# Two plain gate/value pairs instead of three ahead of the Strassen products, and operand-sum words that go through DRAM

## The chip, the core and the metric

The kernel runs on one core of a Trainium2 chip. A core has five engines, each with its own instruction queue: TensorE (PE in the profile, with its weight loads as PEld), VectorE (DVE), ScalarE (ACT), GpSimd (POOL) and SyncE (SP), which here only issues transfers. Engines wait for each other through semaphores. A transfer (DMA) is started by an instruction in an engine's queue and moved by sixteen DMA engines. Matrix products end in PSUM, everything else that the engines read lies in the on-chip memory SBUF, and what doesn't fit there goes to DRAM.

The metric is the time of one execution in microseconds, the median of the runs.

## What is computed

One step of a decoder layer for two groups of requests together: a prompt of 1024 tokens and 8 x 8 sample tokens, so 1088 tokens (T) with a model width of 1024. Cut to what bears on the change, the end of the layer is:

```python
    h = x + merged @ w_out
    up = rmsnorm(h, norm2_g) @ w_up                 # 1024 -> 2 * 2816
    up_ext = jnp.concatenate([conv_f_past, up], axis=1)
    uc = dwconv_valid(up_ext, ffn_conv_w, ffn_conv_b)   # depthwise, 3 steps in time
    gate, val = jnp.split(uc, 2, axis=-1)
    y = h + (jax.nn.silu(gate) * val) @ w_down
```

with `rmsnorm(x, g) = x * rsqrt(mean(x * x) + eps) * g`. Attention, the convolution branch and the input projection come before and are not touched. All of it is fp32.

## The kernel before, in words

**Products.** TensorE multiplies in a reduced format (fp32r), so each fp32 factor is split into a high and a low part, and a product is three matmuls: high weight by high operand, high weight by low operand, low weight by high operand (`mm3`, L188 to L192, which is why the matmuls of the profile stand at L190, L191 and L192). The split is `split_ps` (L224 to L226): ScalarE casts the value into the high part, then VectorE subtracts that from the value to get the low part. Weights come in raw (`wraw`, 512 KB each, loaded on SP's queue by `w_load`) and are split by `w_parts` (L171 on ScalarE, L172 on VectorE) into tiles `whi` and `wlo`.

**The norm.** The output stage (`out`) works in four quarters of 272 tokens (`QUARTERS`). As each quarter of h is finished, `norm2(c)` (L1071) makes one matmul for the mean of squares (L1074), the reciprocal root, and then, for each of eight slices k of 128 model channels, the normed value `nt` (VectorE, L1080; three rotating tiles of 128 x 272) and its split into `mh` (high) and `ml` (low). At its end POOL's queue stores the quarter of h to DRAM (`d_h`). The last quarter's norm is placed 42 priority steps late (`NORM_LATER`), so that it falls inside the first pair of the next stage. The pool `wt`, in which `nt` lies, is closed behind it, and its memory is then free for the pools of the next stage.

**The up stage** (`ffn_up`, L1102) has 22 pairs: the gate unit f and the value unit f, each 128 channels wide. The first `PLAIN` = 3 pairs are plain: two units by four quarters by eight slices by three matmuls, each 272 columns wide, 192 matmuls. The other pairs (`pair`, L1291) take the 2 x 2 block product of Strassen and Winograd with the two weights as one side and two halves of the tokens and of the channels as the other: seven products, each of 24 matmuls, 168. For these, both sides need sums. The operand sums T1 to T4 are made once, by `sums()` (L1222), in four rounds (two halves j by two slices kk). A round builds four words of 128 x 544 in the four rotating tiles `s` (`word`), each of which is the norm's value of two slices for one quarter; then four VectorE operations combine them, and four splits put them in the tiles `th` and `tl`. Before the change, `word` is a VectorE addition that puts the value together again from `mh` and `ml`. `sums()` is called behind the first plain pair, `SUM_LATER` = 60 priority steps late.

The weight sums of a pair are made by `preps` (`plan_pair`, L1250): seven steps a pair, each an optional VectorE sum (L1264, into the same `s` tiles) and a split into one of four ring tiles named `whi0`, `wlo0`, `whi1`, `wlo1` (each holds a high and a low half of 128 x 512). They run three products ahead (`AHEAD`). The seven products use in turn the operands "11", T1, T2, "22", T3, "21", T4.

**Behind a pair**, `finish` (L1175) works on what ScalarE has copied from PSUM into `st` (L1163): `up_conv` writes the edges of the convolution's state with POOL copies, starts the sum on ScalarE (L1170) and adds the two other steps on VectorE (L1172, twice a unit); then Silu, gate times value (L1182, L1185), and a store to DRAM for the down stage (`d_g`, or the parts `d_b` with their differences). The argument `late` of `finish` is in priority steps; the plain pairs pass 0, the others `UP_LATER` = 100, and gate times value another `GATE_LATER` = 60.

**Order.** The program is written in one order and each engine's queue is filled by a scheduler that goes by priority; `later(n)` makes what stands under it n steps less urgent. So a change in one place can move instructions of another engine. Transfers of weights and `word`s wait in SP's queue, in order; stores (`d_h`, `d_g`, `d_b`) and the copies of the key and value caches (`o_kwp`, `o_vwp`, 960 KB each, in `up_start` of unit 2) in POOL's queue, in order. A rotating tile is given again when its last reader is done; a tile in memory that another pool had before waits for that pool's last users, transfers among them.

`raw_slot` and `slot` place weights: the raw weights of every other pair behind the plain ones go to `wraw2`, and the two halves of the last plain unit's weight (the one just before `first`, which follows from `PLAIN`) are put in `wraw2` too, the others in `whi` and `wlo`. The pool `ft`, which holds `wraw2`, `s`, `st` and `acc`, is opened when `wt` is closed.

Of the kernel before, what the change touches and what calls it, by code (L numbers as in the profile page):

```python
# [6 lines left out]
F32 = mybir.dt.float32  # L7
F32R = mybir.dt.float32r
AF = mybir.ActivationFunctionType
ALU = mybir.AluOpType  # L10
AX = mybir.AxisListType

P = 128
DM = 1024
KT = DM // P
# [21 lines left out]
AW = FW - 2  # L37
QW = T // 4
QUARTERS = [(c * QW, QW) for c in range(4)]
PLAIN = 3  # L40
AHEAD = 3
UP_LATER = 100
SUM_LATER = 60
GATE_LATER = 60
DOWN = ((0, 1), (2, 3), (16, 17), (18, 19, 20, 21))
# [75 lines left out]
class Build:  # L121
# [475 lines left out]
    def run(self):  # L597
        nc, tc, a = self.nc, self.tc, self.a
        es = ExitStack()
        with es:  # L600
            dp = es.enter_context(tc.tile_pool(name="dram", bufs=1, space=bass.MemoryType.DRAM))
            self.d_ah = self.t(dp, [4, P, T], "d_ah")
            self.d_al = self.t(dp, [4, P, T], "d_al")
            self.d_c = self.t(dp, [KT, P, T], "d_c")
            self.d_ga = self.t(dp, [KT, P, T], "d_ga")
            self.d_gb = self.t(dp, [KT, P, T], "d_gb")
            self.d_ma = self.t(dp, [KT, P, T], "d_ma")
            self.d_h = self.t(dp, [KT, P, T], "d_h")
            self.d_g = self.t(dp, [NF, P, T], "d_g")
            self.d_b = self.t(dp, [6, 7, P, HALF], "d_b")  # L610
            self.psum = es.enter_context(tc.tile_pool(name="psum", bufs=4, space=bass.MemoryType.PSUM))
            g = es.enter_context(tc.tile_pool(name="g", bufs=1))
            self.wp = es.enter_context(tc.tile_pool(name="w", bufs=2))
            self.consts = self.t(g, [P, CTOT], "consts")
            first = COFF["ident"][0]
            nc.scalar.dma_start(self.consts[:, :first], a["consts"][:, :first])
            self.ident = self.c("ident", 0, P)
            self.mean = self.t(g, [P, P], "mean")
            self.identr = self.t(g, [P, P], "identr", F32R)
            nc.vector.memset(self.mean, 1.0 / DM)  # L620
            self.warm = self.t(g, [P, 1], "warm")
            nc.vector.memset(self.warm, 1.0)
            self.nsink = self.t(g, [P, 16], "nsink")
            self.cb2 = self.t(g, [P, KT], "cb2")
            self.hsum = self.t(g, [P, KT * 16], "hsum")
            self.nsrow = self.t(g, [P, 2], "nsrow")
            ps = self.bank("mm")
            for _ in range(12):
                nc.tensor.matmul(ps[:, 0:P], self.mean, self.mean, start=True, stop=True)
            self.w_raw, self.w_hl, self.w_used, self.w_stop = [], [], 0, len(self.order)  # L630
            self.phase_x()
# [361 lines left out]
    def phase_z(self, s_es, sh, sl):  # L993
        nc, tc, a, pool = self.nc, self.tc, self.a, self.pool
        m_es = ExitStack()
        mp = pool(m_es, "m")

        def quarters():
            make = lambda x: [[self.t(mp, [P, KT // 2, QW], f"m{x}{c}{y}", F32R) for y in range(2)] for c in range(4)]
            return make("h"), make("l")  # L1000

        mh, ml = quarters()
        z_es = ExitStack()
        zt = pool(z_es, "zt")

        def xs(c, k):
            return sh[c][:, k, :], sl[c][:, k, :]

        def do_pb(m):
            t = self.t(zt, [P, T], "gb", bufs=2)  # L1010
            nc.sync.dma_start(t, self.d_gb[m])
            nc.scalar.activation(t, t, AF.Sigmoid)
            r = self.t(zt, [P, T], "mar", bufs=2)
            nc.sync.dma_start(r, self.d_ma[m])

            def ev(c, o, n, ps):
                cs = slice(o, o + n)
                nc.vector.tensor_tensor(t[:, cs], ps[:, :n], t[:, cs], ALU.mult)
                nc.vector.tensor_tensor(r[:, cs], r[:, cs], t[:, cs], ALU.add)
                for z, (qo, qn) in enumerate(QUARTERS):  # L1020
                    lo, hi = max(o, qo), min(o + n, qo + qn)
                    if lo < hi:
                        d = slice(lo - qo, hi - qo)
                        self.split_ps(mh[z][m // 4][:, m % 4, d], ml[z][m // 4][:, m % 4, d], r[:, lo:hi])

            self.stream(("pb", m), xs, ev)

        for m in range(KT):
            do_pb(m)
        z_es.close()  # L1030
        s_es.close()
        h_es = ExitStack()
        hp = pool(h_es, "h", "left")
        H = self.t(hp, [P, KT, T], "H")
        wb = pool(h_es, "wb", "left")
        wt_es = ExitStack()
        wt = pool(wt_es, "wt")
        ssq = [self.t(wt, [P, QW], f"ssq{c}") for c in range(4)]
        n_out = self.order.index(("out", 0))
        tail = n_out + KT - OUT_TAIL  # L1040

        def slot(i):
            if i < n_out:
                return self.wp, i % 2
            if tail <= i < tail + OUT_TAIL:
                return wt, f"t{i - tail}"
            if i >= tail + OUT_TAIL:
                return self.wp, i % 2
            return ((self.wp, 1), (wb, 0), (self.wp, 0))[(i - n_out) % 3]

        self.slot = slot

        def xm(c, k):
            return mh[c][k // 4][:, k % 4, :], ml[c][k // 4][:, k % 4, :]

        def ev_out(m):
            def ev(c, o, n, ps):
                t = self.t(wt, [P, QW], "xr2", bufs=4)
                nc.sync.dma_start(t[:, :n], a["xT"][m, :, o:o + n])
                hs = H[:, m, o:o + n]  # L1060
                nc.vector.tensor_tensor(hs, ps[:, :n], t[:, :n], ALU.add)
                if m == 0:
                    nc.scalar.activation(ssq[c][:, :n], hs, AF.Square)
                else:
                    nc.scalar.activation(t[:, :n], hs, AF.Square)
                    nc.vector.tensor_tensor(ssq[c][:, :n], ssq[c][:, :n], t[:, :n], ALU.add)
            return ev

        hh, hl = [], []

        def norm2(c):  # L1071
            o, n = QUARTERS[c]
            ps = self.bank("aux")
            nc.tensor.matmul(ps[:, :n], self.mean, ssq[c][:, :n], start=True, stop=True)  # L1074
            self.rstd(ssq[c][:, :n], ps[:, :n])
            hh.append([self.t(mp, [P, KT // 2, QW], f"mh{c}{y}", F32R) for y in range(2)])
            hl.append([self.t(mp, [P, KT // 2, QW], f"ml{c}{y}", F32R) for y in range(2)])
            for k in range(KT):
                t = self.t(wt, [P, QW], "nt", bufs=3)
                nc.vector.scalar_tensor_tensor(t[:, :n], H[:, k, o:o + n], self.c("g2", k), ssq[c][:, :n],  # L1080
                                               ALU.mult, ALU.mult)
                self.split_ps(hh[c][k // 4][:, k % 4, :], hl[c][k // 4][:, k % 4, :], t[:, :n])
            nc.gpsimd.dma_start(self.d_h[:, :, o:o + n].rearrange("k p t -> p k t"), H[:, :, o:o + n])

        ms = list(range(KT))
        for m in ms[:-OUT_TAIL]:
            self.stream(("out", m), xm, ev_out(m), table=QUARTERS)
        ws = [self.weight(("out", m), 2) for m in ms[-OUT_TAIL:]]
        for c in range(4):
            for m, w in zip(ms[-OUT_TAIL:], ws):  # L1090
                self.stream(None, xm, ev_out(m), chunks=(c,), w=w, table=QUARTERS)
            with self.later(NORM_LATER[c]):
                norm2(c)
        wt_es.close()
        h_es.close()
        self.gt = {}
        self.ffn_up(hh, hl, mp)
        self.ffn_down(mp)
        m_es.close()


    def ffn_up(self, hh, hl, mp):  # L1102
        nc, tc, a, pool = self.nc, self.tc, self.a, self.pool
# [101 lines left out]
        def plain(f):  # L1205
            fs = (f, NF + f)
            ws = [self.weight(("up", x), 2 - n if f == 0 else 1) for n, x in enumerate(fs)] if f == 0 else [None] * 2
            both = [up_start(x) for x in fs]
# [4 lines left out]
            else:  # L1213
                for x, b in zip(fs, both):
                    self.stream(("up", x), xs, b[3], chunks=range(4), table=QUARTERS)
            finish(f, both, 0)

        def g_raws(n):
            for f in self.groups[n]:
# [2 lines left out]
        def sums():  # L1222
            add = lambda o, x, y, op=ALU.add: nc.vector.tensor_tensor(o, x, y, op)
            for j in range(2):
                for kk in range(0, KT // 2, 2):
                    ks = slice(kk, kk + 2)

                    def word(c, y):
                        r = self.t(ft, [P, 2, QW], "s", bufs=4)
                        add(r, hh[c][y][:, ks].bitcast(F32), hl[c][y][:, ks].bitcast(F32))  # L1230
                        return r

                    r11, r12, r22, r21 = word(j, 0), word(2 + j, 0), word(2 + j, 1), word(j, 1)
# [88 lines left out]

        for f in range(PLAIN, NF):
            plan_pair(f)
# [353 lines left out]
```

## Time and profile before

| | us |
|---|---|
| time, median of three runs | 1666.21 (1664.36 to 1667.17) |
| span of the profiled execution | 1662.4 |
| TensorE busy | 1652.5 (99%) |
| VectorE busy | 1337.3 (80%) |
| ScalarE busy | 866.3 (52%) |
| GpSimd busy | 290.2 (17%) |

The page has no time of the profiled execution other than its span, the time from the first to the last instruction of the trace. TensorE's granted clock is at full speed in every slice of the span, and the DMA engines move 113 GB/s as a mean over it.

How to read the rows: a group of instructions is named by line, engine, operation, the tiles out<-in, and the shapes (partitions x elements); "x16 | 11.5, 721" means sixteen of them, 11.5 us busy together, 721 ns each. Rows of a timeline begin with the start in us from the span's start and the duration in us; several equal instructions in a row are one row, and a bracket at the end gives the idle time of the engine before it and who ended it. Rows of transfers give the size and the us from issue to landing. A matmul's duration is that of its passage through the array; the next one starts long before it is out, so the pace is read from starts.

### The profile page before, as it was taken

Reading aid. Unit: us, or ns where it says so; the run is one execution under the profiler, and the core shown is the slowest. Engines: PE = TensorE matmul, PEld = TensorE weight load, DVE = VectorE, ACT = ScalarE, POOL = GpSimd, SP = SyncE. Lnnn points to the kernel's source line nnn. Section 1 sums busy time; section 2 is a strip of 40 time slices with the busy share of each in tenths; the row PEclk is TensorE's granted clock in tenths of the full one; section 3 lists DMA queues with packets and bytes.
Section 4 is the critical chain, followed back from the end, with each engine's and each line's share of the span. In section 5 each row is a group of like instructions: output and inputs, shape, how many; then the busy total and the mean of one; then the engine's idle time right before and its main releaser. Section 6 shows DMA issues by size and latency. Waiting matters only on the chain.

```text
span 1662.4 us, 29877 instructions
## 1 busy us (share of the span) xinstructions
PE 1652.5 (99%) x11550; PEld 1636.9 (98%) x11550; DVE 1337.3 (80%) x2432; ACT 866.3 (52%) x1781; POOL 290.2 (17%) x483
## 2 busy tenths in 40 slices
PE   9999999999999999999999999999999999999998
PEld 9999999999999999999999999999999999999997
DVE  7899979999989986855545896777887786988867
ACT  6424368774488845973233454444444454524222
POOL 0100112231011111110000171344444320000000
PEclk9999999999999999999999999999999999999999
DMA  6221212232121265544343332244444324766403
GB/s 208 84 71 42 75 60 81 99 103 86 55 53 48 77 227 168 178 154 145 106 155 108 80 125 103 97 113 115 112 114 111 94 103 134 243 168 168 118 14 108
DMA packets 98623, 187.09 MB, mean 113 GB/s; under 512 B 22848, under 2 KB 57680, under 8 KB 98464
## 3 DMA queue, kind: packets, MB, share of 16 engines
q1 hardware_dynamic: 79152, 125.18, 24.3%
q0 software_dynamic: 18896, 59.72, 11.9%
q8 instruction: 91, 1.49, 0.4%
q14 instruction: 52, 0.43, 0.1%
q10 hardware_dynamic: 432, 0.27, 0.1%
HBM read 129.75 MB, written 57.35 MB: 113 GB/s over the span
## 4 chain that ended last, share of the span: by engine, by line
PE 91%; DVE 5%; ACT 2%; DMA 1%; issue 1%; ACTq 0%; DVEq 0%; SPq 0%
PE mm L190 23%; PE mm L192 23%; PE mm L191 23%; PE aux L190 6%; PE aux L192 6%; PE aux L191 6%; PE aux L406 1%; DVE c L520 1%; PE aux L418 1%; PE aux L419 1%; PE aux L396 1%; PE aux L397 1%; DVE bt L520 1%; DVE q L739 1%; DMA bw<-d_b 0%
## 5 line engine op out<-in xcount | busy, mean ns | idle before, releaser
L190 PE MATMUL mm<-xh,whi 128*128 128x384 f32 (+1 forms) x904 | 301.1, 333 | 0.0
L191 PE MATMUL mm<-xl,whi 128*128 128x384 f32 (+1 forms) x904 | 295.4, 327 | 0.1
L192 PE MATMUL mm<-xh,wlo 128*128 128x384 f32 (+1 forms) x904 | 295.4, 327 | 0.0
L191 PEld LDWEIGHTS mm<-xl,whi 128*128 128x128 f32 x904 | 170.0, 188 | 1.6 <-DVE xl L277 0.7
L190 PEld LDWEIGHTS mm<-xh,whi 128*128 128x128 f32 x904 | 169.8, 188 | 0.7
L192 PEld LDWEIGHTS mm<-xh,wlo 128*128 128x128 f32 x904 | 169.7, 188 | 0.1
L190 PE MATMUL mm<-mh,whi 128*128 128x272 f32 (+4 forms) x428 | 125.9, 294 | 0.0
L191 PE MATMUL mm<-ml,whi 128*128 128x272 f32 (+4 forms) x428 | 125.1, 292 | 0.0
L192 PE MATMUL mm<-mh,wlo 128*128 128x272 f32 (+4 forms) x420 | 123.5, 294 | 0.0
L1172 DVE SCALAR_TENSOR_TENSOR acc<-st,fc,acc 128x1104 f32<-128x1104 f32 x88 | 119.8, 1364 | 2.8 <-ACT acc L1170 2.0
L171 ACT CAST whi<-wraw 128x1024 fp32r<-128x1024 f32 (+1 forms) x76 | 74.2, 981 | 79.8 <-PE mm L191 59.7
L520 DVE SCALAR_TENSOR_TENSOR bt<-u,consts,bt 128x513 f32<-128x513 f32 x120 | 89.8, 748 | 0.7
L520 DVE SCALAR_TENSOR_TENSOR c<-sm,hsum,c 128x512 f32<-128x512 f32 x120 | 89.6, 747 | 0.7
L172 DVE TENSOR_TENSOR wlo<-wraw,whi 128x1024 fp32r<-128x1024 f32 (+1 forms) x76 | 86.1, 1136 | 4.9 <-ACT whi L171 4.6
L520 DVE SCALAR_TENSOR_TENSOR c<-u,consts,c 128x512 f32<-128x512 f32 x112 | 83.7, 747 | 0.5
L190 PEld LDWEIGHTS mm<-mh,whi 128*128 128x128 f32 x428 | 80.5, 188 | 0.2
L191 PEld LDWEIGHTS mm<-ml,whi 128*128 128x128 f32 x428 | 80.6, 188 | 0.0
L192 PEld LDWEIGHTS mm<-mh,wlo 128*128 128x128 f32 x420 | 79.0, 188 | 0.0
L1152 POOL COPY st<-co 128x16 f32<-128x16 f32 x44 | 75.6, 1724 | 0.2 <-issue 0.2
L191 PE MATMUL mm<-tl,whi 128*128 128x272 f32 x240 | 69.6, 290 | 0.0
L1320 ACT COPY st<-mm 128x272 f32<-128x272 f32 (+2 forms) x133 | 44.6, 349 | 47.8 <-PE mm L192 47.8
L192 PE MATMUL mm<-th,whi 128*128 128x272 f32 x240 | 69.3, 289 | 0.0
(462 smaller groups left out, 5491.6 us busy)
## 6 DMA issues: line engine op xcount, KB each, us to landing
wraw<-wall SPq DMA_DIRECT2D x118, 512.0 KB, 3.8
bw<-d_b SPq DMA_DIRECT2D x42, 272.0 KB, 3.4
d_b<-gd POOLq DMA_DIRECT2D x36, 272.0 KB, 6.1
d_b<-acc POOLq DMA_DIRECT2D x24, 272.0 KB, 3.3
ar<-wdn SPq DMA_DIRECT2D x32, 192.0 KB, 4.3
d_g<-acc POOLq DMA_DIRECT2D x10, 544.0 KB, 4.3
ga<-d_ga SPq DMA_DIRECT2D x8, 544.0 KB, 4.0
gb<-d_gb SPq DMA_DIRECT2D x8, 544.0 KB, 3.6
```

Of the source, the lines that this page charges most:

```text
L171: self.cast = self.nc.scalar.copy(h[:, z], r[:, z]).ins
L172: self.nc.vector.tensor_tensor(l[:, z], r[:, z], h[:, z].bitcast(F32), ALU.subtract)
L190: mm(ps, wh, xh, start=first, stop=False, skip_group_check=more)
L191: mm(ps, wh, xl, start=False, stop=False, skip_group_check=more)
L192: mm(ps, wl, xh, start=False, stop=last, skip_group_check=more)
L396: nc.tensor.matmul(ps[:, j, :], q[g][:, h, qs], kd[g][:, keys], start=True, stop=False)
L397: nc.tensor.matmul(ps[:, j, :], q[g][:, h, qs], kl[g][:, keys], start=False, stop=True)
L406: nc.tensor.transpose(ps[:, h * P:(h + 1) * P], pt[:, h, kb * P:(kb + 1) * P], self.ident)
L520: mac = lambda o, x, w: nc.vector.scalar_tensor_tensor(o, x, w, o, ALU.mult, ALU.add)
L1152: nc.gpsimd.tensor_copy(ss[:, :, 0:2], co[:, f, 2:].rearrange("p (b t) -> p b t", b=NB))
L1172: nc.vector.scalar_tensor_tensor(acc, st[:, k:k + AW], fw(f, k), acc, ALU.mult, ALU.add)
L1320: op(d, r(ps))
```

## The change

`PLAIN` goes from 3 to 2: the third pair is made by products like the others, and the Strassen pairs begin one pair earlier. `finish` of the plain pairs gets 240 priority steps instead of 0. In `norm2` the normed values are made in tiles of two slices (`nt`, 128 x 2 x 272, four of them), and behind every second slice POOL's queue stores such a tile to a new tensor in DRAM, `d_n`: four stores of 272 KB a quarter, sixteen in all. `word` no longer adds `mh` and `ml`; it loads the value from `d_n` on SP's queue into the tile `s`, sixteen loads of 272 KB. The value is then the norm's fp32 result itself and not the sum of its two parts. The four combinations and four splits of a round stay as they are.

```diff
@@ -37,9 +37,10 @@
-PLAIN = 3
+PLAIN = 2
 AHEAD = 3
 UP_LATER = 100
+PLAIN_LATER = 240
 SUM_LATER = 60
@@ -606,6 +607,7 @@
             self.d_h = self.t(dp, [KT, P, T], "d_h")
+            self.d_n = self.t(dp, [4, KT // 2, P, 2, QW], "d_n")
             self.d_g = self.t(dp, [NF, P, T], "d_g")
@@ -1076,10 +1078,13 @@
             for k in range(KT):
-                t = self.t(wt, [P, QW], "nt", bufs=3)
-                nc.vector.scalar_tensor_tensor(t[:, :n], H[:, k, o:o + n], self.c("g2", k), ssq[c][:, :n],
-                                               ALU.mult, ALU.mult)
-                self.split_ps(hh[c][k // 4][:, k % 4, :], hl[c][k // 4][:, k % 4, :], t[:, :n])
+                if k % 2 == 0:
+                    pair = self.t(wt, [P, 2, QW], "nt", bufs=4)
+                t = pair[:, k % 2, :]
+                nc.vector.scalar_tensor_tensor(t, H[:, k, o:o + n], self.c("g2", k), ssq[c][:, :n], ALU.mult, ALU.mult)
+                self.split_ps(hh[c][k // 4][:, k % 4, :], hl[c][k // 4][:, k % 4, :], t)
+                if k % 2:
+                    nc.gpsimd.dma_start(self.d_n[c, k // 2], pair)
             nc.gpsimd.dma_start(self.d_h[:, :, o:o + n].rearrange("k p t -> p k t"), H[:, :, o:o + n])
@@ -1213,7 +1218,7 @@
-            finish(f, both, 0)
+            finish(f, both, PLAIN_LATER)
@@ -1227,7 +1232,7 @@
                         r = self.t(ft, [P, 2, QW], "s", bufs=4)
-                        add(r, hh[c][y][:, ks].bitcast(F32), hl[c][y][:, ks].bitcast(F32))
+                        nc.sync.dma_start(r, self.d_n[c, (4 * y + kk) // 2])
                         return r
```

The line numbers of the prediction are those of the kernel before.

## The prediction

> **What bounds the kernel now.** I read the page's head and its chain of waits first, then TensorE's own waits from 1000 us on, then the timelines of the stretch that the change touches.
>
> ```profile
> span 1662.4 us, 29877 instructions
> PE 1652.5 (99%) x11550; PEld 1636.9 (98%) x11550; DVE 1337.3 (80%) x2432; ACT 866.3 (52%) x1781; POOL 290.2 (17%) x483
> ...
> PE 91%; DVE 5%; ACT 2%; DMA 1%; issue 1%; ACTq 0%; DVEq 0%; SPq 0%
> ```
>
> ```profile
> PE mm L190 <- DVE H L1456: 0.9, 1, 0.9
> ```
>
> TensorE is never without work: 91% of the chain that ends last is its own matmuls, and in the last 662 us it waits once, for 0.9 us. So time is won by removing matmuls and lost by each wait given to TensorE. The plain pairs and the first product of the first Strassen pair look like this in its timeline (start, duration, instruction):
>
> ```profile
> 929.90 0.29 PE L190 MATMUL mm<-mh,whi 128*128 128x272 f32 x1
> ...
> 1003.19 0.29 PE L190 MATMUL mm<-mh,whi 128*128 128x272 f32 x1
> ...
> 1006.22 0.29 PE L190 MATMUL aux<-th,wlo 128*128 128x272 f32 x1
> ```
>
> The three plain pairs (576 matmuls) run from 929.90 to 1003.19. The first product, 24 matmuls, takes 1006.22 - 1003.19 = 3.03 us, so a matmul costs 0.126 us (the 0.29 is its length in the pipeline), and 576 of them 72.6; the other 0.66 is the fourth quarter's norm matmul, run in two passes inside the first pair. VectorE has to make the operand sums T1 to T4 and the weight sums before 1006.22. It ends that work here:
>
> ```profile
> 942.61 2.62 DVE L1223 TENSOR_TENSOR s<-mh,ml 128x544 f32<-128x544 f32 x4
> 945.15 1.47 DVE L1223 TENSOR_TENSOR s<-s,s 128x544 f32<-128x544 f32 x2
> ...
> 995.19 0.68 DVE L1264 TENSOR_TENSOR s<-wraw,wraw 128x512 f32<-128x512 f32 x1
> 1007.11 0.69 DVE L226 TENSOR_TENSOR whi<-s,whi 128x512 fp32r<-128x512 f32 x1 [11.24 <-ACT whi L225]
> ```
>
> It is busy from the norm's end, 942.6, to 995.9, and then idle for 11.24 us. That is all the slack there is, and the change takes away 24.2 us of the time in which it lies.
>
> **What is removed.** A plain pair is 8 quarters of 24 matmuls, 192; a Strassen pair is 7 products of 24, 168. One pair changes from one to the other: 24 x 0.126 = 3.03 us less on TensorE. This is certain, and it is the largest gain there can be: 0.18%. VectorE loses its word additions and keeps these (view by lines, 930 to 1003 us; busy, mean ns):
>
> ```profile
> L1223 DVE TENSOR_TENSOR s<-s,s 128x544 f32<-128x544 f32 x16 | 11.5, 721 | 0.0
> L226 DVE TENSOR_TENSOR tl<-s,th 128x544 fp32r<-128x544 f32 x16 | 11.1, 722 | 0.0
> L1172 DVE SCALAR_TENSOR_TENSOR acc<-st,fc,acc 128x1104 f32<-128x1104 f32 x8 | 10.8, 1366 | 0.0
> L1223 DVE TENSOR_TENSOR s<-mh,ml 128x544 f32<-128x544 f32 x16 | 10.7, 719 | 0.0
> ...
> L1182 DVE TENSOR_TENSOR acc<-acc,acc 128x1024 f32<-128x1024 f32 x2 | 2.4, 1221 | 0.0
> ```
>
> Back to back a 128x544 operation takes (945.15 - 942.61)/4 = 0.635 us, so 16 additions are 10.2 us. Against 24.2 us of lost time that leaves 14.0 to find, of which 11.2 were idle; the rest is later convolutions (PLAIN_LATER).
>
> **What is added: a round trip through DRAM.** Sixteen stores d_n on POOL's queue, beside the four d_h; sixteen word loads on SP's queue. The nearest rows for their size (272 KB; last column us from issue to landing), and the spread of bw's loads:
>
> ```profile
> wraw<-wall SPq DMA_DIRECT2D x118, 512.0 KB, 3.8
> bw<-d_b SPq DMA_DIRECT2D x42, 272.0 KB, 3.4
> d_b<-gd POOLq DMA_DIRECT2D x36, 272.0 KB, 6.1
> d_b<-acc POOLq DMA_DIRECT2D x24, 272.0 KB, 3.3
> ```
>
> ```profile
> DMA to landing us min/median/max: 2.6/3.4/5.4
> ```
>
> The first twelve stores fall in the output stage, where each of 12 us has room (four norm2 calls, POOL 17% busy): cost 0, at most 1 us if the x loads that share the DMA engines come late. The last quarter decides. Its last norm multiply and the work behind it:
>
> ```profile
> 940.85 0.91 DVE L1080 SCALAR_TENSOR_TENSOR nt<-H,consts,ssq 128x272 f32<-128x272 f32 x2
> ...
> 953.57 1.22 DVE L172 TENSOR_TENSOR wlo<-wraw,whi 128x1024 fp32r<-128x1024 f32 x1
> ```
>
> In the built order of the changed kernel the first VectorE instruction after norm2 is the split of the last plain unit's weight into wraw2. That tile lies where the norm's nt tiles lay, so it waits for the last d_n store. Last multiply done 941.8, store landed 3.3 later: 945.1 (bounds 944.4 with 2.6, 947.9 with 6.1). Split, 1.2: 946.3. On SP's queue the load of the next wraw waits for that split, and three of the first four word loads stand behind it, though their data has long been in DRAM. 512 KB takes 3.8 in the median row and 3.5 on an idle queue (view of DMA, 940 to 960 us):
>
> ```profile
> wraw<-wall SPq DMA_DIRECT2D x2, 512.0 KB, 3.5
> ```
>
> So it lands at 949.8, and the words, half as large, about 0.8 apart behind it: 950.6, 951.4, 952.2. So VectorE idles some 2.5 + 4.3 us where it had four additions (2.5 us): nearly half of the 10.2 saved is given back in the first round.
>
> **Start of the second plain pair.** Then five sums and splits (3.2 us) and the low half of the gate weight (L172, 1.2): from 950.6 on 4.4 us without a gap, 955.0; with some 0.6 of waiting for the second and third word, 955.6. TensorE is done with the first pair at 929.90 + 0.66 + 24.2 = 954.8 and needs that low half 0.25 later: 955.0. Stall +0.6; bounds 0 (loads at 2.6) and 4 (store at 6.1 and loads at their slowest).
>
> **Start of the first product T1.** From 955.6 VectorE's order holds 26 sums and splits of 0.635 (16.5), six convolution steps L1172 of 1.28 (7.7), a gate multiply (L1182, 1.2, and its small remainder) and two weight pieces (0.7 each) ahead of T1's weight: 26.8 us, 982.4. TensorE, begun on that pair at 954.8 + 0.6, gets to T1 at 955.4 + 24.2 + 3.0 = 982.6. Just in time, were that all. But behind it stands one more L1172, of the second pair's value half, which waits for ScalarE, which waits for the last plain matmul:
>
> ```profile
> 952.75 0.44 ACT L1163 COPY st<-mm 128x208 f32<-128x208 f32 x2
> 953.28 1.31 ACT L1170 ACTIVATE acc<-st,fc 128x1104 f32<-128x1104 f32 x1
> 954.49 0.63 ACT L225 CAST th<-s 128x544 fp32r<-128x544 f32 x1
> ...
> 957.76 2.64 DVE L1172 SCALAR_TENSOR_TENSOR acc<-st,fc,acc 128x1104 f32<-128x1104 f32 x2
> 960.32 0.72 DVE L1223 TENSOR_TENSOR s<-s,s 128x544 f32<-128x544 f32 x1
> ...
> 1060.47 0.29 PE L192 MATMUL mm<-th,whi 128*128 128x272 f32 x1
> 1060.80 0.62 ACT L225 CAST whi<-s 128x512 fp32r<-128x512 f32 x1 [2.40 <-PE mm L192]
> 1061.46 0.69 DVE L226 TENSOR_TENSOR whi<-s,whi 128x512 fp32r<-128x512 f32 x1 [0.15 <-ACT whi L225]
> ```
>
> Two steps of L1172 take 960.32 - 957.76 = 2.56, so one is 1.28. ScalarE begins 1060.80 - 1060.47 = 0.33 after the start of the matmul it waits for. The last plain matmul starts 3.0 before T1 is due, at 979.6; then the copy, L1170, a th cast and the weight's cast follow, 0.53 + 1.21 + 0.63 + 0.62 = 3.0 us, so the high half is there at about 982.9 (+0.3). VectorE, free at 982.4, does L1172 (1.28), the last tl (0.64) and the low half (0.69): 985.0, wanted after four matmuls of the high half, 983.4. Stall 0.3 + 1.6 = +1.9, set by the order, hardly by the loads (bounds 1.2 to 2.2).
>
> To this comes what the later word rounds lose. Four s buffers hold one round, so each load waits until its predecessor's word has been split. Rounds 2 and 4 are covered by convolution steps. Round 3 issues at 962 to 966 and meets the cache copies (view of DMA, 960 to 975 us):
>
> ```profile
> o_kwp<-kpT POOLq DMA_DIRECT2D x1, 960.0 KB, 7.2
> o_vwp<-vp POOLq DMA_DIRECT2D x1, 960.0 KB, 10.6
> d_g<-acc POOLq DMA_DIRECT2D x1, 544.0 KB, 9.5
> wraw<-wall SPq DMA_DIRECT2D x1, 512.0 KB, 4.2
> ```
>
> A load of 512 KB took 4.2 us at their end, 3.8 elsewhere. VectorE comes to round 3 at about 968.4. I take +1.0; bounds 0 (all landed) and 4.6 (words only when o_vwp is done, 973).
>
> **In the second Strassen pair** the built order of TensorE runs product "21" directly after T1, not T2. Both weights use the same ring tile (whi0), so TensorE must stand until T1's last matmul is out, the cast (0.62) is done and, four matmuls later, the low half (0.69) too. By the rows above: 0.33 + 0.62 - 0.13 = 0.8, and 0.3 more for the low half (0.15 + 0.69 less four matmuls, 0.5). +1.1 (0.9 to 1.4). The later pairs keep their old order: 0.
>
> **Sum**: -3.0 + 0.6 + 1.9 + 1.0 + 1.1 = +1.6 us; best ends -3.0 + 0 + 1.2 + 0 + 0.9 = -0.9, worst ends together -3.0 + 4 + 2.2 + 4.6 + 1.4 = +9.2. The profiled span goes from 1662.4 to 1664.0; the median of the runs lies 3.8 above that span, and I keep this distance: 1666.2 + 1.6 = **1667.8 us**.
>
> **Rivals.** (1) The stalls are hidden and the matmuls count in full: 1663.2 to 1665. For it: 11.24 us of idle VectorE. Against: T1's low half stands behind work that waits for the last plain matmul, whatever the loads do. (2) Late words: round 3's loads land only as o_vwp ends. From the point where they land after 968.4, each us later is a us on T1: up to 4.6 instead of 1.0, +5.2 in all, 1671.4; with the first round slow as well, 1674. For it: 10.6 and 9.5 us in that window. Against: SP's 512 KB took 4.2. (3) The last d_n store is slow, as d_g's was (9.5 us instead of 3.3): the split, the loads and the second plain pair start 6.2 later, about 3 to 6 of it stay: 1670 to 1673. For it: that d_g was issued at 964.5, amid VectorE's sums. Against: VectorE has 0.8 us of work left and then waits for this very store.
>
> [...]
>
> **How the numbers follow.** Forecast as summed, -0.9 to +3.3: 0.53. Rival 1: 0.13. Rival 2: 0.24. Rival 3: 0.08. Anything else: 0.02. A measurement of this kernel can tell 0.2%, 3.3 us, from no change. Rival 1 hardly gets there (3.0), so faster 0.04; slower takes rivals 2 and 3 and the rest, 0.34; same 0.62. The range leaves out the ends of rival 1 and the worst sums: 1664.8 to 1672.5; the forecast's own is 1665.3 to 1669.5.
>
> **What would show it.** Right: 24 fewer matmuls; TensorE waits for the gate weight near 955 (under 1 us), for wlo at T1 near 982 (about 2.9, round 3's share in it) and for whi after the second pair's T1 near 1008 (about 1.1); VectorE idle from 942.6 to about 950 but for one split. Wrong: no wait of TensorE in 980 to 985 (rival 1), VectorE idle near 968 for over 2 us on s loads (rival 2), or the wraw2 split starting after 947 (rival 3).

## The result, and the profile after

| | before | after |
|---|---|---|
| time, median of five runs each, us | 1665.79 (1664.36 to 1667.17) | 1674.04 (1672.96 to 1678.07) |
| ratio | | 1.0052, 95% interval 1.0040 to 1.0065 |
| span of the profiled execution, us | 1662.4 | 1676.3 |

The changed kernel is 8.25 us slower; 1667.8 was forecast, 1664.8 to 1672.5 was the range. The profiled execution of the changed kernel is the slowest of its five, 4.0 us over the median; that of the kernel before is the fastest. Spans are therefore not compared below, but places.

The page's head and chain of waits of the changed kernel:

```profile
span 1676.3 us, 29931 instructions
PE 1655.6 (99%) x11526; PEld 1639.5 (98%) x11526; DVE 1335.6 (80%) x2433; ACT 868.3 (52%) x1786; POOL 279.2 (17%) x499
...
PE 67%; issue 18%; DVE 7%; DMA 3%; ACT 2%; POOL 2%; SPq 0%; ACTq 0%; DVEq 0%; POOLq 0%
```

The 24 matmuls are gone (11550 to 11526). Yet the chain that ends last runs through TensorE for 67%, not 91%: behind T1 it goes back over a load of words and VectorE to the last d_n store, and from there along POOL's queue. These shares tell where the chain runs and not what it costs: the changed kernel with the copies in pieces, below, has 72% and the same 18% of issue, at 1664.89 us. TensorE's own waits, 900 to 1100 us (total, times, longest), in which the kernel before has none:

```profile
PE aux L191 <- ACT wlo L226: 7.3, 1, 7.3
PE aux L191 <- ACT whi L226: 0.7, 1, 0.7
PE aux L193 <- DVE wlo L227: 0.3, 1, 0.3
```

Lines are one to five numbers higher than before: L191 to L193 are the three matmuls, L226 the cast, L227 the low half. The first and third wait are at T1, the second in the second Strassen pair. TensorE's timeline shows what T1 cost, from the last matmul of the product "11" to the start of T2:

```profile
981.97 0.29 PE L193 MATMUL mm<-mh,whi 128*128 128x272 f32 x1
...
989.53 0.60 PE L191 MATMUL aux<-th,wlo 128*128 128x272 f32 x1 [7.27 <-ACT wlo L226]
...
995.84 0.43 PE L191 MATMUL mm<-th,whi 128*128 128x272 f32 x1
```

T1 was due at 981.97 + 0.13 = 982.1 and began 7.4 late. Its 24 matmuls then took 995.84 - 989.53 = 6.3 us; before, 3.0. The table by stages says why (last columns: granted clock, DMA share, GB/s):

```profile
985.00:989.50 4.50, 0.00 (x0) 0.00 (x0) 4.50 (x7) 4.16 (x9) 1.72 (x2) 0.61 0.55 215
989.50:996.00 6.50, 6.14 (x25) 5.82 (x26) 5.87 (x9) 1.55 (x4) 0.00 (x0) 0.50 0.01 4
996.00:998.00 2.00, 2.00 (x17) 2.00 (x16) 0.41 (x1) 1.93 (x6) 0.00 (x0) 0.94 0.00 0
```

While TensorE waited its clock was taken to half (1.00 over 984 to 986, 0.50 over 986 to 988), and it stayed there until some 7 us after work had come back (0.50 up to 996, 0.94 over 996 to 998): 3.3 us more on T1, in which the 0.3 for the low half lies. So T1 cost 7.4 + 3.3 = 10.7 us, the second pair 0.9, and the saved matmuls are 3.0: +8.6, against +8.25 measured.

This execution loses in one more place. In the down stage, from 1440 us on, TensorE waits 3.6 us in all (0.9 in the kernel before), and its clock is at 0.72 as a mean over 1528 to 1534, which costs 6 x 0.28 = 1.7. Together that is 4.4 us more than before, about what this execution lies over the median; no profile shows what the other four lose there.

Why T1 began late, VectorE shows:

```profile
941.81 0.86 DVE L227 TENSOR_TENSOR ml<-nt,mh 128x272 fp32r<-128x272 f32 x2
944.47 1.23 DVE L173 TENSOR_TENSOR wraw<-wraw,wraw 128x1024 fp32r<-128x1024 f32 x1 [1.81 <-DMA d_n<-nt]
950.32 1.58 DVE L1228 TENSOR_TENSOR s<-s,s 128x544 f32<-128x544 f32 x2 [4.62 <-DMA s<-d_n]
...
953.71 1.22 DVE L173 TENSOR_TENSOR wlo<-wraw,whi 128x1024 fp32r<-128x1024 f32 x1
...
967.08 1.23 DVE L1187 TENSOR_TENSOR acc<-acc,acc 128x1024 f32<-128x1024 f32 x1
974.94 0.73 DVE L1228 TENSOR_TENSOR s<-s,s 128x544 f32<-128x544 f32 x1 [6.63 <-DMA s<-d_n]
...
990.40 0.68 DVE L227 TENSOR_TENSOR wlo<-s,wlo 128x512 fp32r<-128x512 f32 x1
```

It idles 1.81 + 4.62 us ahead of the first round and 6.63 ahead of the third, 13.1 in all, more than the 10.2 us of additions that the loads replace. The view of DMA, 960 to 975 us, names the third round's rival:

```profile
s<-d_n SPq DMA_DIRECT2D x4, 272.0 KB, 10.3
o_kwp<-kpT POOLq DMA_DIRECT2D x1, 960.0 KB, 8.1
o_vwp<-vp POOLq DMA_DIRECT2D x1, 960.0 KB, 12.1
```

Four words of 272 KB took 10.3 us each to land, beside two cache copies.

### The profile page after: what moved, and what is told of

Its sections match the earlier page's. It is cut to its first block, busy times and chain, and to the rows that moved or that the text cites. A ratio compares the mean times of both kernels' runs of the same rounds, so it can differ in the third digit from the quotient of the medians.

```text
span 1676.3 us, 29931 instructions
## 1 busy us (share of the span) xinstructions
PE 1655.6 (99%) x11526; PEld 1639.5 (98%) x11526; DVE 1335.6 (80%) x2433; ACT 868.3 (52%) x1786; POOL 279.2 (17%) x499
## 4 chain that ended last, share of the span: by engine, by line
PE 67%; issue 18%; DVE 7%; DMA 3%; ACT 2%; POOL 2%; SPq 0%; ACTq 0%; DVEq 0%; POOLq 0%
PE mm L191 15%; PE mm L193 15%; PE mm L192 15%; PE aux L193 6%; PE aux L191 6%; PE aux L192 5%; PE aux L407 1%; DMA bw<-d_b 1%; DVE c L521 1%; DMA s<-d_n 1%; PE aux L419 1%; PE aux L420 1%; POOL d_ma L980 1%; PE aux L397 1%; PE aux L398 1%
## 5 line engine op out<-in xcount | busy, mean ns | idle before, releaser
L191 PE MATMUL mm<-xh,whi 128*128 128x384 f32 (+1 forms) x904 | 301.1, 333 | 0.0
L193 PE MATMUL mm<-xh,wlo 128*128 128x384 f32 (+1 forms) x904 | 295.4, 327 | 0.0
L191 PEld LDWEIGHTS mm<-xh,whi 128*128 128x128 f32 x904 | 170.0, 188 | 0.7
L193 PEld LDWEIGHTS mm<-xh,wlo 128*128 128x128 f32 x904 | 169.7, 188 | 0.1
L193 PE MATMUL mm<-mh,wlo 128*128 128x272 f32 (+4 forms) x364 | 107.8, 296 | 0.0
L191 PE MATMUL mm<-mh,whi 128*128 128x272 f32 (+4 forms) x364 | 107.7, 296 | 0.0
L192 PE MATMUL mm<-ml,whi 128*128 128x272 f32 (+4 forms) x364 | 107.0, 294 | 0.0
L1157 POOL COPY st<-co 128x16 f32<-128x16 f32 x44 | 70.9, 1618 | 0.2 <-issue 0.2
L192 PE MATMUL mm<-tl,wlo 128*128 128x272 f32 x240 | 69.5, 290 | 0.0
L193 PE MATMUL mm<-th,wlo 128*128 128x272 f32 x240 | 69.3, 289 | 0.0
L193 PE MATMUL mm<-th,whi 128*128 128x272 f32 x240 | 69.3, 289 | 0.0
L191 PE MATMUL mm<-th,whi 128*128 128x272 f32 x240 | 69.2, 289 | 0.0
```

What stands on the lines that cost most here:

```text
L191: mm(ps, wh, xh, start=first, stop=False, skip_group_check=more)
L192: mm(ps, wh, xl, start=False, stop=False, skip_group_check=more)
L193: mm(ps, wl, xh, start=False, stop=last, skip_group_check=more)
L1157: nc.gpsimd.tensor_copy(ss[:, :, 0:2], co[:, f, 2:].rearrange("p (b t) -> p b t", b=NB))
```

## The experiments

Two theories stood after this reading. Collision: the third round's words wait for the cache copies, which makes T1 late. Rival: the copies are bystanders, and the round trip or the lack of VectorE's time makes T1 late. Times are medians; each ratio, with its 95% interval, is to the kernel before, measured beside the run.

**The cache copies moved to unit 8, in the changed kernel and in the one before.**

```diff
-            if f == 2:
+            if f == 8:
                 with tc.issue_after(z.ins):
                     nc.gpsimd.dma_start(a["o_kwp"], a["kpT"][:, :, :, NT:])
```

Changed kernel:

> The changed kernel with the two cache copies (o_kwp, o_vwp, 960 KB each) issued in unit 8 instead of unit 2; all else as changed. Theory A (collision: the third round's word loads, issued at 962 to 966 us, share the DMA engines with these copies and land only when o_vwp does): the third round's loads land 2.6 to 4 us after issue instead of 10.3, VectorE idles under 1.5 us before it instead of 6.6, T1 waits 1 to 2.5 us instead of 7.3, TensorE's clock stays full behind it; time 1674.0 - 5.5 - 2.6 - 0.5 = about 1665.5 (1664 to 1667). Rival B (the copies are bystanders: the round trip, the wait for the last d_n store and VectorE's order make T1 late by themselves): T1 waits 5 us or more and the time stays at 1671 or above.

Measured: 1671.62, ratio 1.0032 (1.0019 to 1.0044). The view of DMA, 960 to 975 us, and the waits of VectorE and TensorE around it:

```profile
s<-d_n SPq DMA_DIRECT2D x8, 272.0 KB, 2.8
```

```profile
DVE s L1228 <- DMA s<-d_n: 4.7, 2, 4.4
DVE wraw L173 <- DMA d_n<-nt: 1.8, 1, 1.8
```

```profile
PE aux L191 <- ACT wlo L226: 0.8, 1, 0.8
PE aux L193 <- DVE wlo L227: 0.8, 1, 0.8
```

With the copies gone the words land in 2.8 us instead of 10.3, VectorE's wait for words falls from 11.2 us to 4.7 (the first round's) and T1's wait from 7.6 to 1.6. VectorE does the same work ahead of T1's weight in both kernels, with seven convolution steps among it, and has the weight ready at 984.4 instead of 991.1. That is the collision, as expected. But the time is 6 us above what was expected. 1.7 of these are the clock, at 0.57 from 984 to 988 behind T1's two waits of 0.8, and TensorE waits another 3.7 us in the pair behind unit 8. The control shows most of the latter without the change.

Kernel before:

> The kernel before, with the same move of the two cache copies to unit 8. Control: in the kernel before nothing waits for transfers in that window, so both theories expect 1665.8 within 1 us. If it is faster by more than 1 us, the gain of the other run is not that of the words.

Measured: 1670.71, ratio 1.0028 (1.0018 to 1.0039): the control moved by 4.6 us. Its waits of TensorE, 1125 to 1160 us, in the pair behind unit 8:

```profile
PE mm L190 <- ACT st L1320: 2.2, 1, 2.2
PE aux L190 <- ACT wlo L225: 0.7, 1, 0.7
```

Without a word from DRAM in the kernel, TensorE waits 2.9 us there, and the clock falls to 0.57 for the next 4 us (4 x 0.43 = 1.7 us): 4.6 in all. In the built orders of TensorE the pair behind the copies has the product "21" ahead of T2, on a weight tile that is not free yet. The changed kernel has this in its second pair, the one behind unit 2. In the kernel before, whose unit 2 is plain, the order is whole. So moving the copies moved this break as well.

**One part of the change at a time.** The words through DRAM with three plain pairs (`PLAIN = 3` in the changed kernel):

> The changed kernel with PLAIN back at 3: words through DRAM, three plain pairs. Theory A: the words are as late as in the changed kernel (third round near 974 to 976), but T1 is due 24 us later, so it does not wait; 1665.8 within 1.2 us. Rival B2 (the sixteen stores and loads cost time by themselves, in the output stage or by contention): 1668 or more. Neither expects a gain, since TensorE has no waits to lose here.

Measured: 1667.46, ratio 1.0007 (0.9998 to 1.0016). TensorE waits 0.7 + 0.2 us behind T1, where the built order again has "21" early. So of the 1.3 us, which the interval doesn't tell from nothing, 0.9 are that order, and with slack the stores and loads as such are nearly free.

Two plain pairs with the words still added (`PLAIN = 2`, `PLAIN_LATER = 240` in the kernel before):

> The kernel before with PLAIN = 2 and PLAIN_LATER = 240: the words stay VectorE additions, no stores and loads of d_n. From durations: VectorE has 10.2 us of additions more than in the changed kernel but no waits for words, so it is through with T1's weight at about 942.6 + 45.4 = 988.0, where 983.4 is wanted. Theory A: T1 waits 4 to 6 us, the clock dips shortly; time 1665.8 - 3.0 + 5 + 1 to 2.5 + 0.9 = 1669.5 to 1671.5, which is faster than the changed kernel: the additions would have been cheaper than the loads that meet the copies. Rival B: the additions cost more than the loads, 1674 or more.

Measured: 1670.43, ratio 1.0025 (1.0015 to 1.0035). The number is that of theory A, but for another reason. TensorE's waits, 940 to 1030 us:

```profile
PE mm L191 <- ACT st L1321: 2.2, 1, 2.2
PE aux L191 <- ACT whi L226: 0.8, 1, 0.8
```

Both are in the second pair (1006 and 1010 us). At T1 there is no wait at all: my sum, by which the additions end at 988, was wrong, since the scheduler put the later convolution steps behind T1's weight: three stand ahead of it, where the changed kernel has seven and a gate multiply. VectorE had the time; what this kernel lacks is TensorE's order. It also repeats the collision with another victim: two weight loads of 512 KB beside the copies (view of DMA, 983 to 1000 us):

```profile
wraw<-wall SPq DMA_DIRECT2D x2, 512.0 KB, 8.1
o_kwp<-kpT POOLq DMA_DIRECT2D x1, 960.0 KB, 7.3
o_vwp<-vp POOLq DMA_DIRECT2D x1, 960.0 KB, 11.0
```

**The copies early, behind the third quarter's store of h.** New theory C: the changed kernel loses by collision and by broken order, not by a lack of VectorE's time. The edit takes the copies out of unit 2 and puts them into `norm2`:

```diff
-            nc.gpsimd.dma_start(self.d_h[:, :, o:o + n].rearrange("k p t -> p k t"), H[:, :, o:o + n])
+            z = nc.gpsimd.dma_start(self.d_h[:, :, o:o + n].rearrange("k p t -> p k t"), H[:, :, o:o + n])
+            if c == 2:
+                with self.tc.issue_after(z.ins):
+                    nc.gpsimd.dma_start(self.a["o_kwp"], self.a["kpT"][:, :, :, NT:])
+                    nc.gpsimd.dma_start(self.a["o_vwp"], self.a["vp"][:, NT:, :])
```

> The kernel before with PLAIN = 2, PLAIN_LATER = 240 (words still VectorE additions) and the two cache copies issued on POOL's queue behind the third quarter's store of h (about 926 us), not in unit 2. Theory C (what the two-pair kernel with additions lost was not VectorE's time but TensorE's order in the second Strassen pair, which the built order breaks in the pair behind the one that issues the copies): no wait of TensorE at T1 nor in the second pair, no clock dip; the 24 matmuls count in full: 1666.0 - 3.0 = 1663.0 (1662 to 1664.5). Rival D (two plain pairs are too short a time for the sums, wherever the copies are): waits at T1 or behind it stay, 1666 or more.

> The changed kernel (words through DRAM) with the same move of the cache copies to behind the third quarter's store of h. Theory C: no load of words meets the copies (they land by about 941), the second pair's order is whole, and in this built order no convolution step stands ahead of T1's weight: VectorE is through at about 980.6, T1 is due at 982, so no wait: 1663.0 (1662 to 1665); VectorE still idles some 6.4 us before the first round (wait for the last d_n store, then for the words). Rival E (the round trip through DRAM costs TensorE time by itself): a wait of 1 us or more at 955 or T1, 1665 to 1668.

> Control: the kernel before (three plain pairs, additions) with the cache copies behind the third quarter's store of h. Both theories: 1666.0 within 1 us, since there is no wait that the copies cause in the kernel before. If this is faster, the gain of the other two is partly that of the place of the copies.

Measured: 1677.68, 1668.05 and 1677.16; ratios 1.0067 (1.0055 to 1.0080), 1.0011 (1.0002 to 1.0020) and 1.0064 (1.0051 to 1.0078). None came out as expected. The control alone loses 10.5 us, so this set says nothing on two against three pairs. The copies were issued at 919, not 926, and met the load of the convolution states `co`. Its row in the control (view of DMA, 918 to 925 us), and who waited in the end (waits of POOL 925 to 966, of TensorE 940 to 970):

```profile
co<-cfT SPq DMA_DIRECT2D x1, 352.0 KB, 16.3
```

```profile
POOL st L1152 <- DMA co<-cfT: 15.6, 1, 15.6
```

```profile
PE mm L190 <- ACT st L1163: 8.7, 2, 7.3
```

In the kernel before the same row ends in 8.9:

```profile
co<-cfT SPq DMA_DIRECT2D x1, 352.0 KB, 8.9
```

It is the collision a third time, on a load that nobody had thought urgent. Two plain pairs with additions wait for it too, 9.6 us at T1. The changed kernel has whole order and no copies at 960, and no wait at T1, but it doesn't show what theory C wanted. It waits 1.3 + 0.9 us at the start of the second plain pair, where VectorE waited 3.6 us for the last d_n store and 4.9 for words; that is the sign of rival E. The clock falls behind these waits (0.72 as a mean over 956 to 962), so TensorE comes to T1 only at 986.2. And only four convolution steps stand ahead of T1's weight there, not seven. Its `co` took 24.1 us to land, so the copies were no bystanders here either.

**The copies in eight pieces, one a unit in units 4 to 11.** With this TensorE's built order is whole in all kernels:

```diff
-            if f == 2:
+            if 4 <= f < 12:
                 with tc.issue_after(z.ins):
-                    nc.gpsimd.dma_start(a["o_kwp"], a["kpT"][:, :, :, NT:])
-                    nc.gpsimd.dma_start(a["o_vwp"], a["vp"][:, NT:, :])
+                    nc.gpsimd.dma_start(a["o_kwp"][:, :, f - 4], a["kpT"][:, :, f - 4, NT:])
+                    nc.gpsimd.dma_start(a["o_vwp"][f - 4], a["vp"][f - 4, NT:, :])
```

> Control: the kernel before with the cache copies in eight pieces in units 4 to 11: 1666.4 within 1 us. If it moves by more, the pieces themselves cost or gain.

> The kernel before with PLAIN = 2, PLAIN_LATER = 240 (words stay VectorE additions), the cache copies cut into eight pieces of 240 KB that are issued one a unit in units 4 to 11, so that none holds the DMA engines for more than some 2 us. Theory C (two plain pairs with additions are long enough for the sums; what was lost was the order behind the copies and the collisions with them): no wait of TensorE at T1 or in the second pair, no clock dip, -3.0: 1663.4 (1662.5 to 1665). Rival D (the additions don't fit into two plain pairs): T1 waits over 1 us, 1666 or more.

> The changed kernel with the cache copies in eight pieces in units 4 to 11; one convolution step still stands ahead of T1's weight in VectorE's order, as in the changed kernel. No collision in the third round; T1 waits about 1.6 us in all, as it did with the copies in unit 8, and the clock dips for some us behind that (1.7): 1666.4 - 3.0 + 1.6 + 1.7 = 1666.7 (1665.5 to 1668). If instead the time stays at 1669 or above, something else of the change costs that I have not found.

> As a_spread with PLAIN_LATER = 100, by which in the built order the convolution step of the second pair's value half comes behind T1's weight. Theory C: T1 waits 0 to 0.5 us, no dip, 1663.4 (1662.5 to 1665). The difference to a_spread is the price of that one step ahead of T1's weight: about 3 us expected, half of it clock. Rival: no difference, then T1's lateness comes from the words alone.

| | time, us | ratio, 95% interval |
|---|---|---|
| control, three plain pairs, additions | 1666.08 | 1.0000 (0.9991 to 1.0009) |
| two plain pairs, additions | 1663.10 | 0.9982 (0.9973 to 0.9991) |
| two plain pairs, words through DRAM | 1664.89 | 0.9998 (0.9990 to 1.0007) |
| the same with `PLAIN_LATER = 100` | 1665.68 | 0.9999 (0.9990 to 1.0008) |

The control stands still. Two plain pairs with additions gain 2.7 us, nearly all of the 3.0 that 24 matmuls are worth, and TensorE has no wait from 900 us to the end of the up stage. VectorE ends T1's weight just in time (timelines of VectorE and TensorE):

```profile
981.33 0.68 DVE L227 TENSOR_TENSOR wlo<-s,wlo 128x512 fp32r<-128x512 f32 x1
```

```profile
982.13 0.29 PE L191 MATMUL aux<-th,wlo 128*128 128x272 f32 x1
```

With words through DRAM T1 still waits, in the run with 240:

```profile
PE aux L193 <- DVE wlo L227: 0.8, 1, 0.8
PE aux L191 <- ACT wlo L226: 0.6, 1, 0.6
```

With 100 it waits 1.0 + 0.4, just as long, though one convolution step fewer stands ahead of T1's weight there. So moving that step alone gained nothing, against what I expected; the built order put a weight sum (0.68 us) ahead in its place, and the weight is ready at 984.1 instead of 984.0. After these waits the clock stayed full (1.00 in every 2 us from 980 to 990), against what I expected too.

The kernels with additions and with words through DRAM differ in more than the words, since the scheduler fills VectorE's queue anew each time. Convolution steps ahead of T1's weight, with additions and with words (views of VectorE's lines from 942 us to the end of that weight, at 982 and 984):

```profile
L1173 DVE SCALAR_TENSOR_TENSOR acc<-st,fc,acc 128x1104 f32<-128x1104 f32 x3 | 4.1, 1360 | 0.0
```

```profile
L1177 DVE SCALAR_TENSOR_TENSOR acc<-st,fc,acc 128x1104 f32<-128x1104 f32 x7 | 9.5, 1361 | 0.0
```

**The first round added again.** VectorE's waits ahead of the first round are nearly the same in the changed kernel and in both kernels with pieces: 1.8 for the last d_n store, 4.4 to 4.6 for the words. The last run takes them out:

```diff
-                        nc.sync.dma_start(r, self.d_n[c, (4 * y + kk) // 2])
+                        if j == 0 and kk == 0:
+                            add(r, hh[c][y][:, ks].bitcast(F32), hl[c][y][:, ks].bitcast(F32))
+                        else:
+                            nc.sync.dma_start(r, self.d_n[c, (4 * y + kk) // 2])
```

> As a_spread, with the four words of the first round made by VectorE additions again and the other twelve loaded through DRAM. Theory F (what is left of T1's wait, 1.4 us in both runs with the pieces, is VectorE's idle time before the first round, 1.8 us for the last d_n store and 4.7 us for the words that stand on SP's queue behind the next weight; the step ahead of T1's weight is not the price): the idle time ends with the first round, VectorE is through with T1's weight some 4 us sooner, no wait at T1: 1663.1 (1662.3 to 1664.3), the same as with all words added. Rival G (the later rounds' loads make T1 late): T1 still waits 1 us or more, 1664.5 or more.

Measured: 1663.45, ratio 0.9986 (0.9977 to 0.9995), and TensorE has no wait from 940 to 1003 us. VectorE's waits for transfers in that time are down to one line:

```profile
DVE s L1228 <- DMA s<-d_n: 1.0, 1, 1.0
```

The number is that of theory F. Rival G had little for it: with all words loaded and the copies in pieces, VectorE's waits for words are 4.4 + 0.35 us, both in the first round. But the run doesn't show that the idle time was the cause, for the built order changed as well:

```profile
L1177 DVE SCALAR_TENSOR_TENSOR acc<-st,fc,acc 128x1104 f32<-128x1104 f32 x4 | 5.4, 1354 | 0.0
```

Against the run with all words loaded VectorE idles 5.5 us less and adds 2.6 us of additions, a gain of 2.9, and three convolution steps have gone behind T1's weight, another 4.1. T1's wait was 1.4, so either could have ended it. The version that beats both kernels is two plain pairs with the copies in pieces; all words added (1663.1) or only the first round's (1663.45) cannot be told apart, and the former is the simpler one, without `d_n`.

## Why the prediction was wrong

- **24 x 0.126 = 3.0 us less on TensorE**: right. Two plain pairs with additions and pieces gain 2.7.
- **Round 3, "+1.0; bounds 0 and 4.6"**: this step failed. VectorE came to it at 968.3, as predicted (968.4), and then idled 6.63 us; the words landed only with o_vwp, which itself took 12.1 us beside them and not 10.6. The reason for the 1.0 was the row "wraw, 512 KB, 4.2" in the copies' window. That load was issued at 971.1, when o_kwp had landed and o_vwp had 1.6 us to go, so it had hardly met them. The nearest row was d_g's 9.5, issued in their midst, though on the copies' own queue, and I gave it to rival 3. On T1 the third round cost some 6 us: its wait was 7.6, and 1.6 with the copies in unit 8. Rival 2 was the right one, and dearer than its price of 1671.4. That its other figure, 1674, is the measured one is luck: it took a slow first round, which was not slow.
- **No term for the clock**: the second failure. A wait of 7 us was priced at 7 us, and 3.3 us came on top while T1 ran at a clock of 0.50 (less the 0.3 for the low half). T1's waits were forecast at 2.9 and came to 7.7, which with the clock's 3.0 is 7.8 more; the second plain pair and the second Strassen pair took 0.8 less than forecast. That makes +8.6 of +1.6, in the one profile that there is.
- **"VectorE idles some 2.5 + 4.3 us" ahead of the first round**: right, 1.81 + 4.62.
- **Start of the second plain pair, +0.6**: the low half of the gate weight was done at 953.71 + 1.22 = 954.93 and wanted at 955.0; no wait. Within its bounds.
- **T1's +1.9, "set by the order, hardly by the loads"**: the size was near (1.6 with the copies in unit 8, 1.4 with pieces), and so was the way to it: seven convolution steps ahead of the weight, which was ready at 984.0 with pieces, where 985.0 was forecast. Whether order or loads are to blame stays open. One step fewer gained nothing; with the first round added the wait went, but with three steps fewer. An estimate speaks for the order: with the copies early, four steps and all words loaded, the weight was ready at 983.1 after 8.5 us of idle time; with the usual 6.4 that would be 981.0, before T1 is due.
- **Second Strassen pair, +1.1**: 0.7 of waiting, 0.9 from start to start. Right in place, a little less in size. What the prediction did not see is that the order breaks in the pair behind the copies: it does in five of the six kernels that issue them whole within a unit, all but the kernel before, and in none of the others.
- **Rival 3, the last d_n store**: the split started at 944.47, so the store took 2.4 us. No run here bears out that VectorE's sums slow such a store: d_g's 9.5 us was the copies, for in the changed kernel with the copies in unit 8 a d_g store amid VectorE's sums took 4.5.

The mechanism of the collision, as far as it is shown: the loads on SP's queue (q1) and the copies on POOL's (q0) took their time from the same sixteen DMA engines. In the changed kernel from 964.6 to 974.0 us both queues moved data at once (packets, MB, share of the sixteen engines' time):

```profile
q0 software_dynamic: 176, 1.41, 44.6%
q1 hardware_dynamic: 534, 1.04, 35.4%
```

From 966 to 968 us alone the shares are 57.7% and 40.9%, 98.6% together, so the engines had next to no time left over there. What sets the shares stays open (the packets are 176 against 534). So does the scheduler's reason for the broken order, which was read from the built orders and the waits and not tried by itself.

## What to carry to other kernels

Before a computation is replaced by a load, look at every transfer that is in flight at the time when it will be issued, and price the load by a row of the same queue that was issued in their midst, not at their end (here a word took 10.3 us beside the copies and 2.8 without them). Look too at where large copies stand that nobody waits for: cut into pieces and spread over eight units they cost nothing here (1666.08), and the same edit then cost nothing measurable (0.9998) instead of 8 us. Compare the order of every engine's queue between two kernels before their difference is put down to the edit; here it changed in most runs. And when a bound engine is given a wait of several microseconds, count what it takes until it is back at full pace (here 3.0 us on top of a wait of 7.3).

## What the runs showed that I had not expected

TensorE's granted clock fell to half in some waits or behind them and came back some microseconds later. The wait of 7.3 us in the changed kernel left 6.5 us of work at 0.50. Short waits went either way. Waits of 0.6 and 0.8 us at T1, in the changed kernel with pieces, left no trace (1.00 over 981 to 993); two of 0.8, in the one with the copies in unit 8, left 0.57 over 984 to 988. Around 2 us it is the same: behind 2.2 us the clock was at 0.57 for 4 us in the kernel before with the copies in unit 8, and at 1.00 in the changed kernel with the same wait in the same place (windows of the two kernels behind it):

```profile
1144.00:1148.00 4.00, 4.00 (x22) 4.00 (x21) 4.00 (x6) 2.81 (x6) 1.22 (x2) 0.57 0.00 0
```

```profile
1144.00:1150.00 6.00, 6.00 (x50) 6.00 (x49) 6.00 (x9) 4.00 (x8) 1.75 (x4) 1.00 0.00 0
```

What decides whether the clock falls behind a wait of 2.2 us or less, no run here shows.
